# Four modulation halves summed on VectorE: from column-by-column accumulation to dot products along the partition

## The chip, the cores and the metric

The kernel runs on one core of a Trainium2 chip. The metric is device time in microseconds (us) of one execution. TensorE (PE in the rows, PEld for its weight loads), VectorE (DVE), ScalarE (ACT), GpSimd (POOL) and SyncE (SP, which here issues most of the DMAs) run side by side and wait for each other through semaphores.

## The reference, cut to what matters

A two-layer model on 256 tokens of width 1024. Each layer's norms and residuals are scaled by six vectors of length 1024 that come from one condition vector `c` through a 1024 x 6144 matrix:

```python
c_act = jax.nn.silu(c)
for l in range(DEPTH):
    mod = c_act @ mod_w[l] + mod_b[l]
    sh1, sc1, g1, sh2, sc2, g2 = jnp.split(mod[:, None, :], 6, axis=-1)
    hm = rmsnorm(x, norm_mix_g[l]) * (1.0 + sc1) + sh1
    y = mixer_hgrn2_shortconv(hm, ...) if l % 2 == 0 else mixer_nsa(hm, ...)
    x = x + g1 * y
    hf = rmsnorm(x, norm_ffn_g[l]) * (1.0 + sc2) + sh2
    x = x + g2 * conv_ffn(hf, ...)
return rmsnorm(x, final_norm_g)
```

Everything is float32. Each of the six vectors is 1024 dot products of length 1024, from 4 MB of weights. The program makes one vector at a time, by a function called `mod_half`, so a half here means one such vector. The change concerns four of the twelve: layer 0's `g2`, layer 1's `sc1` and `g1`, and layer 1's `sh2`.

## The kernel before

Activations lie transposed, 8 tiles of 128 features by 256 tokens. All large weights stream through one ring of six 1 MB buffers (`raw_w`, `raw_m`), loaded by SP in the order in which the program uses them; a load is issued when a buffer comes free. A weight matrix product is done in three passes: ScalarE rounds the weights to a high part (`whi`, L156), VectorE subtracts to get the low part (`wlo`, L165), and TensorE multiplies high by high, high by low and low by high (L417, tile `pg`). The splits run up to three sub-tiles ahead of the matmuls. The feed-forward of layer 0 (`ffn`, about 170 to 361 us) is 22 such "up" groups and four "down" groups; the attention of layer 1 (about 365 to 506 us) has its own sequence.

Work that is not part of these products stands in a list, `side`, of small functions. At every sub-tile `slot()` adds a credit (0.6 in the up groups, 1.2 in the down groups) and runs one function for each whole credit. The order of all engines follows from the order in which the program calls things.

A modulation half is made by `mod_half` in one of two ways. With `on_pe=True`, TensorE multiplies the activated condition with the weights (L289, tile `pm`), ScalarE copies the row of sums (L316), four transposes turn it into columns (L321) and VectorE adds the bias (L325, L327). With `on_pe=False`, eight VectorE instructions accumulate weight rows times the condition into `macc`, 128 partitions x 1024 columns (L299 for the first, L301 for the seven others). Then two matmuls with a column of ones add the 128 partitions up (`sums`, L309), and the same row copy (here 64 partitions), four transposes and bias add follow. In `side` that is 8 + 2 empty + `sums`, `rows`, empty, `turn`, `add`: 15 entries. Three halves of this kind stand in the feed-forward of layer 0 (L944), the fourth in the attention (L1288), where the eight steps are called at the iterations 15 to 19 of its loop (1, 1, 2, 2, 2) and the rest between the last output groups (L1330).

At the program's start TensorE runs five warm-up matmuls (`warm`, L627, each two records in the profile), then the first modulation column (L342), then the sums of squares (L484) of the input `xT` that arrives by DMA. `ident`, the identity for transposes, is a part of `kf`, loaded by the first DMA on ScalarE's queue (L240).

Of the kernel before, what the change touches and what calls it, by code (L numbers as in the profile page):

```python
# [38 lines left out]
WARM = (5, 1, 3)  # L39
# [160 lines left out]
def model(ctx, tc, xt, pack, wts, rel_bias, k_f, k_mask, k_hot, out, plan, got):  # L200
# [60 lines left out]
    ccol = one.tile([P, KD], F32, name="ccol")  # L261
    table(AF.Silu)
# [7 lines left out]
    def mod_half(l, qa, qb, on_pe=True, sums_in=None, tag="m"):  # L270
# [22 lines left out]
        def dve_step(j, e):  # L293
            if e == 0:
                s_["r"] = load(j)
            raw = s_["r"]
            if j + e == 0:
                s_["a"] = sums_in()
                dve.tensor_scalar(s_["a"], raw[:, 0, :], ccol[:, 0:1], None, op0=OP.mult)  # L299
            else:  # L300
                dve.scalar_tensor_tensor(s_["a"], raw[:, e, :], ccol[:, 2 * j + e:2 * j + e + 1], s_["a"], op0=OP.mult,  # L301
                                         op1=OP.add)
            if e == 1:
                st.done(s_["i"])

        def sums():
            s_["p"] = ps.tile([P, 512], "pm", "m")
            for q in range(2):
                pe.matmul(s_["p"][32 * q:32 * q + 32, :], one32, s_["a"][:, q * 512:(q + 1) * 512],  # L309
                          start=True, stop=True, skip_group_check=True, tile_position=(0, 32 * q))  # L310

        n = P if on_pe else 64

        def rows():
            s_["w"] = tmp.tile([P, 512], F32, name="mrow", bufs=1)
            act.activation(s_["w"][:n], s_["p"][:n], AF.Copy)  # L316

        def turn():
            s_["t"] = ps.tile([P, 4, P], "pm2", "m")
            for i in range(4):  # L320
                pe.transpose(s_["t"][:, i, :n], s_["w"][:n, i * P:(i + 1) * P], ident[:n, :n])  # L321

        def add():
            pv = s_["t"].rearrange("p j (e q r) -> p e q j r", q=2, r=32)
            dve.tensor_tensor(dst, pv[:, 0, :, :, 0], bias, op=OP.add)  # L325
            if on_pe:
                dve.tensor_tensor(dst, pv[:, 1, :, :, 0], dst, op=OP.add)  # L327
        if on_pe:
            return [lambda j=j: pe_step(j) for j in range(4)] + [rows, nop, turn, add]
        return [lambda j=j, e=e: dve_step(j, e) for j in range(4) for e in range(2)] + [nop] * 2 + [sums, rows, nop, turn, add]  # L330
# [476 lines left out]
    for b in (4, 6, 8):  # L807
        side.extend(mod_half(0, b, b + 1))
# [75 lines left out]
    ffp = [None]  # L884

    def ffn(l, H, rest, extra=None):
        with tc.tile_pool(name=f"ff{l}", bufs=1) as ff:
            ffp[0] = ff
# [54 lines left out]
    for l, b in ((0, 5), (1, 1), (1, 2)):  # L943
        side.extend(mod_half(l, 2 * b, 2 * b + 1, False, lambda: ffp[0].tile([P, 1024], F32, name="macc", bufs=1)))  # L944
# [242 lines left out]
    gT = tmp.tile([48, S], F32, name="gT", tag="m1k", bufs=1)  # L1187
# [9 lines left out]
    hid = tmp.tile([P, 256], F32, name="hid", tag="m1k", bufs=1)  # L1197
# [17 lines left out]
    hT = tmp.tile([P, 2, P], F32, name="hT", bufs=1)  # L1215
    dve.tensor_copy(hT, pt[:, :256].rearrange("p (j n) -> p j n", j=2))
    hv = tmp.tile([P, 2, 4, 4, 16], F32, name="hv", bufs=1)
# [20 lines left out]
    v4 = tmp.tile([64, 4, 64], F32, name="v4", tag="m1k", bufs=1)  # L1238
# [20 lines left out]

    def late_sums():  # L1260
        return ns.tile([P, 4, 400], F32, name="macc", tag="FDM", bufs=2).rearrange("p a n -> p (a n)")[:, :D]
# [3 lines left out]
    for n in range(NH + 6):  # L1265
# [21 lines left out]
        if n == M_AT:  # L1287
            mods = [f for f in mod_half(1, 6, 7, False, late_sums) if f is not nop]  # L1288
# [43 lines left out]
    gap.extend(mod_half(1, 10, 11, True))  # L1332
# [42 lines left out]
def lay_out(inp, plan):  # L1375
# [18 lines left out]
    for kind, off, n, what in plan[0]:  # L1394
        dst = wts[off:off + P * n]
        if what[0] == "mod":
# [42 lines left out]
```

## Time and profile before

| | us |
|---|---|
| median of 3 runs | 704.21 (703.83 to 705.22) |
| the profiled execution | 708.95 |
| its span, to which the rows' times refer | 707.1 |

| engine | busy share of the span |
|---|---|
| TensorE, matmuls | 98% |
| TensorE, weight loads | 90% |
| VectorE | 69% |
| ScalarE | 53% |
| GpSimd | 7% |

The page gives busy time by engine, the chain of work that ended last, groups of instructions by line, and DMA issues; the trace is read further by stretches of time, by instruction and by waits. An instruction's duration includes its tail, in which the next one may already run, so the distance between two starts is shorter than the duration. Times in rows count from the start of the span.

### The profile page before, as it was taken

The numbers are of one execution on the slowest core, as the hardware profiler recorded it, in microseconds if no ns is written. First come the engines' busy times: TensorE is split into PE (matmuls) and PEld (weight loads), VectorE is DVE, ScalarE is ACT, GpSimd is POOL, SyncE is SP. The second block draws the span as 40 slices with busy tenths as digits, with TensorE's granted clock in tenths as the row PEclk, the third lists the DMA queues.
The fourth block names the chain that finished last, engine by engine and source line by source line (L and its number), as shares of the span: only waits on it lengthen the run. The fifth ranks groups of instructions, "written<-read, shape, count | busy, mean of one in ns | idle before, by whom it ended". The sixth has DMA issues, their size and how long they took to land.

```text
span 707.1 us, 14267 instructions
## 1 busy us (share of the span) xinstructions
PE 692.3 (98%) x5866; PEld 637.1 (90%) x5866; DVE 487.1 (69%) x887; ACT 377.1 (53%) x646; POOL 48.1 (7%) x80
## 2 busy tenths in 40 slices
PE   7999999999999999999999999999999999999996
PEld 4889897887999999999989799878789999999996
DVE  2667675548689868969568767788686776775552
ACT  5446235535655555444346668784466555564452
POOL 0000000000000000000010015665000000000000
PEclk8999999999999999999999999999999999999999
DMA  8995657887658856769768482516677555455301
GB/s 332 416 420 211 259 187 251 321 317 285 230 185 296 309 181 246 283 233 337 284 239 319 191 341 81 205 49 224 243 280 266 190 208 199 164 173 193 127 1 60
DMA packets 27794, 165.12 MB, mean 233 GB/s; under 512 B 3258, under 2 KB 3770, under 8 KB 10320
## 3 DMA queue, kind: packets, MB, share of 16 engines
q1 hardware_dynamic: 26352, 159.94, 61.0%
q0 software_dynamic: 944, 3.60, 1.5%
q8 instruction: 46, 0.75, 0.4%
q10 hardware_dynamic: 432, 0.66, 0.2%
q14 instruction: 20, 0.16, 0.1%
HBM read 163.10 MB, written 1.08 MB: 232 GB/s over the span
## 4 chain that ended last, share of the span: by engine, by line
PE 89%; DVE 3%; ACT 3%; DMA 2%; issue 1%; POOL 0%; SPq 0%; ACTq 0%
PE pg L417 74%; PE pm L289 3%; PE pl L726 2%; DMA raw_w<-in_wts_dram 1%; PE pn L484 1%; PE p L1036 1%; DVE wlo L165 1%; PE po L1066 1%; PE pc L1174 1%; PE pm L342 1%; DMA xT<-in_xt_dram 1%; PE sc L988 1%; ACT whi L156 1%; ACT E L1020 1%; PE pm L309 1%
## 5 line engine op out<-in xcount | busy, mean ns | idle before, releaser
L165 DVE TENSOR_TENSOR wlo<-raw_w,whi 128x1024 fp32r<-128x1024 f32 (+1 forms) x194 | 226.3, 1173 | 136.2 <-ACT whi L156 127.4
L417 PE MATMUL pg<-hhi,whi 128*128 128x256 f32 x1096 | 295.8, 284 | 0.1
L417 PE MATMUL pg<-hlo,whi 128*128 128x256 f32 x1096 | 289.1, 278 | 0.0
L417 PE MATMUL pg<-hhi,wlo 128*128 128x256 f32 x1096 | 286.1, 278 | 0.0
L156 ACT ACTIVATE whi<-raw_w 128x1024 fp32r<-128x1024 f32 (+1 forms) x194 | 196.1, 1018 | 146.3 <-PE pg L417 116.9
L417 PEld LDWEIGHTS pg<-hhi,whi 128*128 128x128 f32 x1096 | 200.3, 189 | 19.2 <-issue 12.5
L417 PEld LDWEIGHTS pg<-hlo,whi 128*128 128x128 f32 x1096 | 199.5, 188 | 0.0
L417 PEld LDWEIGHTS pg<-hhi,wlo 128*128 128x128 f32 x1096 | 198.6, 189 | 0.0
L417 PE MATMUL pg<-Ah,whi 128*128 128x256 f32 x352 | 97.9, 278 | 0.0
L417 PE MATMUL pg<-Ah,wlo 128*128 128x256 f32 x352 | 97.2, 276 | 0.0
L417 PE MATMUL pg<-Al,whi 128*128 128x256 f32 x352 | 97.2, 276 | 0.0
L417 PEld LDWEIGHTS pg<-Ah,whi 128*128 128x128 f32 x352 | 66.1, 188 | 1.8 <-ACT whi L156 1.7
L417 PEld LDWEIGHTS pg<-Al,whi 128*128 128x128 f32 x352 | 66.1, 188 | 0.0
L417 PEld LDWEIGHTS pg<-Ah,wlo 128*128 128x128 f32 x352 | 66.1, 188 | 0.0
L1027 POOL TENSOR_SCALAR E<-E,rr,gr 128x128 f32<-128x128 f32 (+1 forms) x64 | 41.1, 657 | 31.0 <-DVE rr L1025 22.7
L902 DVE SCALAR_TENSOR_TENSOR tt<-pg,pk,tt 128x255 f32<-128x255 f32 (+1 forms) x88 | 36.2, 473 | 2.9 <-ACT tt L898 2.9
L912 ACT ACTIVATE Ah<-tt 128x512 fp32r<-128x512 f32 x22 | 13.9, 633 | 44.5 <-DVE tt L911 44.5
L301 DVE SCALAR_TENSOR_TENSOR macc<-raw_m,ccol,macc 128x1024 f32<-128x1024 f32 x28 | 35.9, 1283 | 0.1
L529 ACT ACTIVATE hhi<-xn,modc 128x256 fp32r<-128x256 f32 x31 | 15.1, 507 | 25.0 <-DVE xn L528 25.0
L1020 ACT ACTIVATE E<-E,mx 128x128 f32<-128x128 f32 (+1 forms) x64 | 28.2, 445 | 0.0
L289 PE MATMUL pm<-raw_m,cst 128*32 128x512 f32 x192 | 27.1, 642 | 0.0
L557 DVE SCALAR_TENSOR_TENSOR xT<-pg,modc,xT 128x256 f32<-128x256 f32 x32 | 14.1, 476 | 9.6 <-PE pg L417 9.5
(233 smaller groups left out, 787.3 us busy)
## 6 DMA issues: line engine op xcount, KB each, us to landing
raw_w<-in_wts_dram SPq DMA_DIRECT2D x84, 1024.0 KB, 4.9
raw_m<-in_wts_dram SPq DMA_DIRECT2D x52, 1024.0 KB, 6.6
raw_e<-in_wts_dram SPq DMA_DIRECT2D x24, 256.0 KB, 8.6
raw_w<-in_wts_dram SPq DMA_DIRECT2D x8, 768.0 KB, 4.9
FDM<-ub POOLq DMA_DIRECT2D x4, 800.0 KB, 7.9
raw_w<-in_wts_dram SPq DMA_DIRECT2D x5, 512.0 KB, 5.3
xT<-in_xt_dram SPq DMA_DIRECT2D x3, 256.0 KB, 6.4
out_dram<-yo ACTq DMA_DIRECT2D x2, 256.0 KB, 2.8
```

The lines of the kernel that those rows point to most:

```text
L156: self.nc.scalar.activation(hi, raw, AF.Copy)
L165: self.nc.vector.tensor_tensor(lo, raw, hi, op=OP.subtract)
L289: pe.matmul(s_["p"][o:o + 32, :], cst[:, 2 * j + e, :], raw[:, e, q * 512:(q + 1) * 512], start=(j == 0), stop=(j == 3), skip_group_check= ...
L301: dve.scalar_tensor_tensor(s_["a"], raw[:, e, :], ccol[:, 2 * j + e:2 * j + e + 1], s_["a"], op0=OP.mult, op1=OP.add)
L417: pe.matmul(o, a, b, start=self.first[i], stop=False, skip_group_check=True)
L529: act.activation(hi[:, k, :], xs[k], AF.Identity, bias=B[:, k:k + 1])
L557: dve.scalar_tensor_tensor(xT[:, k, :], src, g[:, k:k + 1], xT[:, k, :], op0=OP.mult, op1=OP.add)
L726: pe.matmul(pp[:, hd, :], lhs[:, hd, ls * P:(ls + 1) * P], rhs[:, hd, rs * P:(rs + 1) * P], start=True, stop=True)
L902: dve.scalar_tensor_tensor(tt[:, m, d:], acc[:, m, :S - d], w_fc[l][:, c:c + 1], tt[:, m, d:], op0=OP.mult, op1=OP.add)
L912: act.activation(Ah[:, sl, :], tt, AF.Copy)
L1020: act.activation(o, o, AF.Exp, bias=E["mx"][:, t, br:br + 1], scale=-1.0, accum_out=E["den"][:, t, br:br + 1])
L1027: pool.tensor_scalar(o, o, rr[:, t, br:br + 1], gr4[:, t, 1 + br, n:n + 1], op0=OP.mult, op1=OP.mult)
```

## The change

The four halves with `on_pe=False` are replaced by `mod_dots`. The weights of these halves are laid out transposed on the host: a partition holds whole columns of the matrix, 1024 elements each, so that one VectorE instruction, `tensor_tensor_reduce`, multiplies such a column with the condition vector, adds the products up along the partition, starts from the bias and writes one column of `modc`. Eight instructions make a half. Each is two instructions for the engine: the product and sum, and a read of the accumulator. The `sums`, `rows`, `turn` and `add` of these halves are gone, and so are `macc` and the empty entries: 8 entries in `side` instead of 15.

For this the condition must lie on every partition as a row of 1024 (`cb`). Eight transposes of a broadcast column, at the very start, and two ScalarE copies make it. The first group of warm-up matmuls goes from five to three. Five small tiles of the attention that shared one buffer (`m1k`) or had their own in `tmp` move to the four buffers of tag `T`.

```diff
-WARM = (5, 1, 3)
+WARM = (3, 1, 3)
...
+    cb = one.tile([P, D], F32, name="cb")
...
-        return [lambda j=j, e=e: dve_step(j, e) for j in range(4) for e in range(2)] + [nop] * 2 + [sums, rows, nop, turn, add]
+    def mod_dots(l, q):
+
+        s_ = {}
+
+        def dot(j, e):
+            if e == 0:
+                s_["i"] = st.load("m", 2048, "dots", l, 512 * q + 256 * j)
+            raw = st.raw(s_["i"])[:, e * D:(e + 1) * D]
+            n = 4 * q + 2 * j + e
+            dve.tensor_tensor_reduce(raw, raw, cb, scale=1.0, scalar=modb[l][:, n:n + 1], op0=OP.mult, op1=OP.add,
+                                     accum_out=modc[l][:, n:n + 1])
+            if e == 1:
+                st.done(s_["i"])
+        return [lambda j=j, e=e: dot(j, e) for j in range(4) for e in range(2)]
...
+    pcb = [ps.tile([P, 4, P], "pcb", "g") for _ in range(2)]
+    for k in range(KD):
+        pe.transpose(pcb[k // 4][:, k % 4, :], ccol[:, k:k + 1].to_broadcast([P, P]), ident)
+    for h in range(2):
+        act.activation(cb[:, h * 512:(h + 1) * 512], pcb[h].rearrange("p k n -> p (k n)"), AF.Copy)
     warm(WARM[0])
...
-    for l, b in ((0, 5), (1, 1), (1, 2)):
-        side.extend(mod_half(l, 2 * b, 2 * b + 1, False, lambda: ffp[0].tile([P, 1024], F32, name="macc", bufs=1)))
+    for l, q in ((0, 10), (1, 2), (1, 4)):
+        side.extend(mod_dots(l, q))
...
-    gT = tmp.tile([48, S], F32, name="gT", tag="m1k", bufs=1)
+    gT = ns.tile([48, S], F32, name="gT", tag="T", bufs=4)
...
-            mods = [f for f in mod_half(1, 6, 7, False, late_sums) if f is not nop]
+            mods = mod_dots(1, 6)
...
+        if what[0] == "dots":
+            _, l, c0 = what
+            dst.reshape(P, 2, D)[...] = f["mod_w"][l][:, c0:c0 + 2 * P].T.reshape(2, P, D).transpose(1, 0, 2)
```

On TensorE, in the feed-forward of layer 0, this is the place between two up groups where the first half's sums stood (`pg` is a group's accumulator, `hhi` and `hlo` the activations; the numbers are the buffers'). Before:

```order
L417 MATMUL pg_2797<-hlo_1937,whi_2729 128x256
L417 MATMUL pg_2797<-hhi_1936,wlo_2730 128x256
L309 MATMUL pm_2873<-macc_2369,one32_131 32x512 x2
L417 MATMUL pg_2798<-hhi_1936,whi_2768 128x256
L417 MATMUL pg_2798<-hlo_1937,whi_2768 128x256
```

and after:

```order
L409 MATMUL pg_2807<-hlo_1948,whi_2739 128x256
L409 MATMUL pg_2807<-hhi_1947,wlo_2740 128x256
L409 MATMUL pg_2808<-hhi_1947,whi_2778 128x256
L409 MATMUL pg_2808<-hlo_1948,whi_2778 128x256
L409 MATMUL pg_2808<-hhi_1947,wlo_2779 128x256
```

The next group now follows directly; nothing else is in a different order on TensorE there. The four transposes of L321 go in the same way at each half's later place.

On VectorE, at the first two steps of the same half (`tt` and `Al` belong to the feed-forward's own gating), before:

```order
L165 TENSOR_TENSOR wlo<-raw_w,whi 128x1024
L299 TENSOR_SCALAR macc<-raw_m,ccol 128x1024
L165 TENSOR_TENSOR wlo<-raw_w,whi 128x1024
L911 TENSOR_TENSOR tt<-pg,tt 128x512
L301 SCALAR_TENSOR_TENSOR macc<-raw_m,ccol,macc 128x1024
L165 TENSOR_TENSOR wlo<-raw_w,whi 128x1024
```

and after:

```order
L165 TENSOR_TENSOR wlo<-raw_w,whi 128x1024
L318 ISA raw_m,modc_81<-raw_m,cb,pk 128x1024
L318 ISA modc_81 128x1
L165 TENSOR_TENSOR wlo<-raw_w,whi 128x1024
L905 TENSOR_TENSOR tt<-pg,tt 128x512
L318 ISA raw_m,modc_81<-raw_m,cb,pk 128x1024
L318 ISA modc_81 128x1
L165 TENSOR_TENSOR wlo<-raw_w,whi 128x1024
```

Each step became a pair in the same place (L318 is `tensor_tensor_reduce`, with the accumulator read behind it). The steps of the second and third half move up, since the seven other entries between the halves are gone: all 24 now stand inside the up groups.

On ScalarE at the start, before:

```order
L264 ACTIVATE ccol<-pk 128x8
L245 ACT_TABLE_LOAD
L245 ACTIVATE scr<-epsc 128x1
L634 ACTIVATE qf<-xT 128x512 x2
L634 ACTIVATE tq<-xT 128x512
```

and after:

```order
L265 ACTIVATE ccol<-pk 128x8
L245 ACT_TABLE_LOAD
L245 ACTIVATE scr<-epsc 128x1
L625 ACTIVATE cb<-pcb 128x512 x2
L632 ACTIVATE qf<-xT 128x512 x2
```

The two copies of the condition stand ahead of the squares of the input.

## Rows read from the trace of the kernel before

**Rows 1.** The page: engines' busy time; shares of the chain that ended last.

```profile
PE 692.3 (98%) x5866; PEld 637.1 (90%) x5866; DVE 487.1 (69%) x887; ACT 377.1 (53%) x646; POOL 48.1 (7%) x80
...
PE 89%; DVE 3%; ACT 3%; DMA 2%; issue 1%; POOL 0%; SPq 0%; ACTq 0%
```

**Rows 2.** Chain that ended last, in order of time (start us, us, what): L309.

```profile
246.13 0.98 PE pm L309 x4
...
502.18 0.98 PE pm L309 x4
```

**Rows 3.** The same chain, asked narrowly around two halves: the transposes.

```profile
255.79 0.39 PE pm L321 x4
...
504.74 0.39 PE pm L321 x4
```

**Rows 4.** Stretches: us, PE, PEld, DVE, ACT, POOL busy (count), PEclk, DMA share, GB/s.

```profile
206.10:240.60 34.50, 34.50 (x295) 34.50 (x295) 30.34 (x38) 18.59 (x25) 0.00 (x0) 1.00 0.76 278
...
314.00:332.00 18.00, 18.00 (x161) 18.00 (x160) 17.21 (x18) 7.86 (x9) 0.00 (x0) 1.00 0.84 313
...
475.90:496.80 20.90, 20.75 (x189) 18.18 (x188) 18.15 (x31) 9.02 (x22) 11.11 (x12) 1.00 0.58 207
```

**Rows 5.** VectorE groups by line and shape: busy us, mean ns | idle before.

```profile
L165 DVE TENSOR_TENSOR wlo<-raw_w,whi 128x1024 fp32r<-128x1024 f32 x176 | 214.1, 1223 | 130.6 <-ACT whi L156 122.0 <-PE pm L321 3.6 <-PE pm L289 3.1
L301 DVE SCALAR_TENSOR_TENSOR macc<-raw_m,ccol,macc 128x1024 f32<-128x1024 f32 x28 | 35.9, 1283 | 0.1
...
L299 DVE TENSOR_SCALAR macc<-raw_m,ccol 128x1024 f32<-128x1024 f32 x4 | 3.0, 740 | 0.0
```

**Rows 6.** VectorE in order of time (start us, us): `tensor_tensor_reduce` in attention.

```profile
472.16 0.29 DVE L1008 CUSTOM_DVE_ANT_0 E<-sc,FDM 128x128 f32<-128x128 f32 x1
...
472.37 0.42 DVE L1008 CUSTOM_DVE_ANT_0 E<-sc,FDM 128x256 f32<-128x256 f32 x1
472.71 0.08 DVE L1008 DVE_READ_ACCUMULATOR2_ANT mx<- 128x1 f32 x1
472.71 0.42 DVE L1008 CUSTOM_DVE_ANT_0 E<-sc,FDM 128x256 f32<-128x256 f32 x1
```

**Rows 7.** VectorE in order of time: the attention's half, first and last steps.

```profile
475.93 0.72 DVE L299 TENSOR_SCALAR macc<-raw_m,ccol 128x1024 f32<-128x1024 f32 x1
477.29 1.22 DVE L165 TENSOR_TENSOR wlo<-raw_w,whi 128x1024 fp32r<-128x1024 f32 x1 [0.64 <-ACT whi L156]
...
492.62 2.60 DVE L301 SCALAR_TENSOR_TENSOR macc<-raw_m,ccol,macc 128x1024 f32<-128x1024 f32 x2
495.13 1.28 DVE L165 TENSOR_TENSOR wlo<-raw_w,whi 128x512 fp32r<-128x512 f32 x2
496.34 0.41 DVE L1053 COPY Tc<-p 64x256 f32<-64x256 f32 x1
```

**Rows 8.** TensorE in order of time, behind those steps.

```profile
496.80 1.08 PE L1091 MATMUL po<-Tc,vc 64*64 64x256 f32 x8 [0.15 <-DVE Tc L1053]
```

**Rows 9.** The chain's first piece.

```profile
2.59 6.63 DMA xT<-in_xt_dram
```

**Rows 10.** TensorE in order of time, at the start.

```profile
3.12 4.05 PE L627 MATMUL pw<-kk,cst 128*32 128x256 f32 x9 [3.12 <-ACT cst L263]
...
10.20 0.44 PE L353 MATMUL pm<-kf,mrow 128*128 128x128 f32 x2 [0.54 <-ACT mrow L348]
```

**Rows 11.** ScalarE in order of time, at the start.

```profile
7.93 1.28 ACT L634 ACTIVATE qf<-xT 128x512 f32<-128x512 f32 x2 [3.26 <-DMA xT<-in_xt_dram]
```

**Rows 12.** The row copies' line: ns min/median/max, first and last start, shapes.

```profile
L316 ACT ACTIVATE mrow<-pm x10: 574/581/600, 99.6 to 532.9; 128x512 f32<-128x512 f32 x6, 64x512 f32<-64x512 f32 x4
```

**Rows 13.** DMA issues: count, KB each, us to landing.

```profile
kf<-in_k_f_dram ACTq DMA_DIRECT2D x1, 130.5 KB, 2.3
```

**Rows 14.** Stretches at the start, columns as in rows 4.

```profile
11.00:12.00 1.00, 1.00 (x7) 0.92 (x6) 0.55 (x5) 0.00 (x0) 0.00 (x0) 0.51 1.10 449
...
17.50:18.00 0.50, 0.50 (x4) 0.50 (x5) 0.50 (x2) 0.00 (x0) 0.00 (x0) 0.66 0.91 377
```

More of the change, by code (lines that the diff above doesn't have):

```diff
@@ L268, in nop, with mod_half @@
         pass
-    def mod_half(l, qa, qb, on_pe=True, sums_in=None, tag="m"):
+    def mod_half(l, qa, qb, tag="m"):
         def cols(t):
@@ L291, in pe_step @@
             st.done(s_["i"])
[L293 to L312, printed above, removed]
         def rows():
             s_["w"] = tmp.tile([P, 512], F32, name="mrow", bufs=1)
-            act.activation(s_["w"][:n], s_["p"][:n], AF.Copy)
+            act.activation(s_["w"], s_["p"], AF.Copy)
         def turn():
@@ L320, in turn @@
             for i in range(4):
-                pe.transpose(s_["t"][:, i, :n], s_["w"][:n, i * P:(i + 1) * P], ident[:n, :n])
+                pe.transpose(s_["t"][:, i, :], s_["w"][:, i * P:(i + 1) * P], ident)
         def add():
@@ L325, in add @@
             dve.tensor_tensor(dst, pv[:, 0, :, :, 0], bias, op=OP.add)
[L326 to L329, printed above, removed]
-        return [lambda j=j, e=e: dve_step(j, e) for j in range(4) for e in range(2)] + [nop] * 2 + [sums, rows, nop, turn, add]
+            dve.tensor_tensor(dst, pv[:, 1, :, :, 0], dst, op=OP.add)
+        return [lambda j=j: pe_step(j) for j in range(4)] + [rows, nop, turn, add]
+    def mod_dots(l, q):
[10 more added lines that the diff above has]
+        return [lambda j=j, e=e: dot(j, e) for j in range(4) for e in range(2)]
     def first_scales(c, A, gb):
@@ L806, in model @@
     after = [None]
-    for b in (4, 6, 8):
-        side.extend(mod_half(0, b, b + 1))
+    side.extend(mod_half(0, 4, 5) + mod_half(0, 6, 7) + mod_half(0, 8, 9))
     side[:0] = [nop] * 3
@@ L1196, in model @@
         pe.transpose(pt3[:, t * 64:t * 64 + 48], gT[:, (1 - t) * P:(2 - t) * P], ident[:48, :48])
-    hid = tmp.tile([P, 256], F32, name="hid", tag="m1k", bufs=1)
+    hid = ns.tile([P, 256], F32, name="hid", tag="T", bufs=4)
     act.activation(hid, pc[:, :256], AF.Silu)
@@ L1331, in model @@
             mods.pop(0)()
-    gap.extend(mod_half(1, 10, 11, True))
+    gap.extend(mod_half(1, 10, 11))
     out_tail(G[3], [G[3].sub(6, 2, HELD_NSA[3])], g1)
@@ L1395, in lay_out @@
         dst = wts[off:off + P * n]
-        if what[0] == "mod":
+        if what[0] == "dots":
+            _, l, c0 = what
+            dst.reshape(P, 2, D)[...] = f["mod_w"][l][:, c0:c0 + 2 * P].T.reshape(2, P, D).transpose(1, 0, 2)
+        elif what[0] == "mod":
             _, l, k, nk, starts, w = what
```

10 lines of the change are left out of this document (3 added, 7 removed).

## Prediction

> **What bounds the kernel now.** I read the page first: TensorE is busy 98% of the span and carries 89% of the chain of work that ended last [rows 1]. So an instruction on TensorE is worth its own time wherever TensorE has no gap, and one on VectorE (69%) or ScalarE (53%) is worth nothing until somebody waits for it. Then the chain in order of time, for the pieces that the change removes: each of the four halves is in it twice, with its two matmuls of sums for 0.98 us and with its four transposes for 0.39 us, of which the first and the last stand here [rows 2, 3]. Last, the stretches in which the eight VectorE steps of a half run. In 206.1 to 240.6 TensorE is busy 34.50 of 34.50 us although VectorE is busy 30.34; in 314 to 332 it is still 18.00 of 18.00 with VectorE at 17.21 of 18 [rows 4]. In the attention, 475.9 to 496.8, TensorE loses 0.15 us, and that one gap ends with VectorE [rows 4, 8].
>
> **What is removed from TensorE.** Four times 0.98 + 0.39 = 5.48 us. These pieces lie between dense matmuls: in the feed-forward no gap stands on either side, so the next group's matmuls start earlier by the whole amount if its weights are split by then. The splits run up to three sub-tiles ahead and TensorE doesn't wait for them in these stretches, so I count all of it: **-5.48 us**. The four row copies (0.58 us each, [rows 12]) and four small adds vanish from ScalarE and VectorE; nobody on the chain waits for them, so they count nothing.
>
> **What VectorE does instead.** The old steps are one L299 and seven L301, 0.72 us and, start to start, 1.26 us (492.62 to 495.13 is two of them) [rows 5, 7]; with the add, about 9.6 us a half. The new instruction of this size is not in the trace. The nearest row is the same instruction in the attention, with a different pair of operations and one source in PSUM: 0.21 us from start to start at 128 columns, 0.34 at 256, and the accumulator read starts together with the next product, so it adds nothing [rows 6]. That is about 1.05 ns a column: 0.34 + 768 x 0.00105 = 1.15 us at 1024 columns, 9.2 us a half. The other end is L301's pace plus a whole accumulator read, 1.26 + 0.08 = 1.34 us, 10.7 us a half. I take 1.15, since it comes from the same instruction.
>
> In the feed-forward this changes a half by -0.4 to +1.1 us in a stretch with 4.2 us of VectorE idle [rows 4], and TensorE runs up to three sub-tiles behind the splits: **0 us**. What is new there is that the three halves follow each other without a pause, 24 steps in a row. Since one half at this density cost no TensorE time, and 314 to 332, in which VectorE was 96% busy, cost none either, I expect no debt to pile up. If the cover went, the price would be the overrun of VectorE. The loads come denser too, with the same bytes: the dense stretch moves 278 GB/s and the one at 314 to 332 313 GB/s, both without a gap on TensorE [rows 4]. A load of weights that is queued on SP behind a load of the modulation would be what is late; no row shows it late at these rates.
>
> In the attention the steps stay at their places. The first grows from 0.72 to 1.15 or 1.34 us, and the split behind it waited 0.64 us for ScalarE anyway [rows 7]. The last four stand right before the splits and the copy `Tc` that TensorE waited for at 496.80. At 1.15 they end earlier and win back at most that 0.15 us; at 1.34 the four add 0.3 us on TensorE's path. I take **0**, with -0.15 to +0.3 as bounds.
>
> **The start.** Two warm-up matmuls less are four records; nine took 4.05 us, tail included, so about 0.43 each and 1.7 us less [rows 10]. Eight transposes are added: at the price of the four in the feed-forward (0.39 us for 64 rows, [rows 3]) 0.8 us, at that of L353 (two in 0.44 us with the tail, [rows 10]) 1.8 us. So TensorE's block at the start moves by -0.9 to +0.1 us. It is under cover in any case: the chain there is the DMA of `xT`, which lands at 9.22 [rows 9], and TensorE has 0.54 us of idle before 10.20 [rows 10]. The two copies into `cb` cost ScalarE two times 0.58 us ([rows 12], the same shape) and stand ahead of the squares, but ScalarE idles 3.26 us there before the input lands [rows 11]. The transposes wait for `kf`: it takes 2.3 us to land [rows 13] as the first transfer on its queue, about when the old warm-up began (3.12, [rows 10]). If it landed late, the copies would first use up ScalarE's 2.1 us of spare idle, and only then push the squares. **0 us**, with bounds of -0.5 and +1.
>
> The renaming of five small tiles in the attention only changes buffers; `hid` no longer waits for the reads of `gT`. TensorE is the chain there and nothing waits for `hid` at once: 0.
>
> **The sum.** -5.48 + 0 + 0 + 0 = -5.5 us on a span of 707.1. The profiled execution took 708.95 us, its span and 1.85 us around it, and the median of the runs is 704.21, 4.7 us below; I carry that distance over unchanged: 704.21 - 5.5 = **698.7 us**.
>
> **Rivals.**
>
> *The new instruction runs at half pace.* Both its sources lie in SBUF as float32, and it sums while it multiplies; the instruction of [rows 6] has one source in PSUM, so the trace doesn't show this combination. For it speaks that L301, with two float32 sources in SBUF, is slower than the subtraction L165 (1283 against 1223 ns, [rows 5]); against it, that this is 5%, not double. Half pace is another 1024 x 1.05 ns: 2.23 us a step, 0.97 more than L301. In the dense stretch eight steps add 7.8 us where 4.2 are idle, an overrun of 3.6 us a half and 10.8 us for three, of which the lead of three sub-tiles (about 8 us) can hide a part once: 2.5 to 10.8 us. In the attention 8 x 0.97 + 0.5 = 8.2 us meet 2.75 us of idle [rows 4]: 5.5 us. Sum: -5.5 + 5.5 + (2.5 to 10.8), **about 710 us, slower**. It decides from roughly 1.8 us a step (1.26 + 4.2/8), and the sum is positive from about 2.1.
>
> [...]
>
> *The gain comes back as a wait in the feed-forward.* The denser steps or loads make one split late per group, TensorE waits instead of multiplying the sums, and only the attention's half or less is won: **about 703.5 us**. For it: VectorE at 88% and DMA at 0.76 over 103 us instead of 35. Against it: the gapless 314 to 332 [rows 4].
>
> [...]
>
> **Chances.** Forecast 0.76 at 698.7 (its own terms span 697.5 to 700.1); clock for the worse 0.07, for the better 0.04; gain comes back 0.06; half pace 0.07. Range: 696.9 to 702.0, which takes in the forecast with its bounds and both clock cases and leaves out 0.13 and the edges. About 0.2%, 1.4 us, is what a measurement of this kernel can tell from no change. Faster by more than that (below 702.8): 0.76 + 0.07 + 0.04 = 0.87 and a little of the gain that comes back, 0.88; same 0.05; slower 0.07.
>
> **What would show it.** No `pm` matmuls from ones and no 64-row transposes in the chain, and TensorE still gapless in the feed-forward. VectorE's new instruction at 1.15 to 1.34 us from start to start; above 1.8 the forecast falls. In the attention, no wait above 0.5 us on VectorE at the copy `Tc`. At the start the squares still begin when `xT` lands, and the first `pg` matmul stands near 17.2 us. A first `pg` matmul later than 18.5, or gaps on TensorE ended by `wlo` or `raw_w` in the feed-forward, would make the prediction wrong.

## The result and the profile after

| | before | after |
|---|---|---|
| median, first comparison | 704.02 us (702.63 to 705.22) | 695.02 us (693.98 to 697.17) |
| the profiled execution | 708.95 us | 697.17 us |
| its span | 707.1 us | 695.4 us |

The ratio is 0.986, 95% interval 0.9826 to 0.9895: faster by 9.0 us by the medians, where the prediction had 5.5, and 1.9 us below the low end of its range. The changed kernel was measured unchanged in two later batches, on two chips: 697.4 (ratio 0.9901, 0.9881 to 0.9920) and 699.2 (0.9921, 0.9895 to 0.9947). Over all 22 runs of the three its median is 697.4, and single runs lie between 694.0 and 702.6; over all 132 runs of before that stood beside the experiments the median is 704.5. So the change is worth about 7 us, and the first four runs lay on the favourable side of its spread, by luck. Medians and ranges here leave out five runs over 1.5% above the fastest of their kernel, one of them of 1144.8 us at a granted clock of 0.56.

Of the changed kernel, the page's lines that answer to [rows 1]:

```profile
PE 680.7 (98%) x5838; PEld 631.4 (91%) x5838; DVE 489.2 (70%) x915; ACT 375.4 (54%) x644; POOL 48.4 (7%) x80
...
PE 90%; DVE 4%; ACT 3%; DMA 1%; issue 0%; POOL 0%; SPq 0%; ACTq 0%
```

TensorE is still the bound. The chain that ended last, in the feed-forward of layer 0 (start us, us, what; the dense matmuls are L409 now, L417 before):

```profile
168.60 13.94 PE pg L409 x120
...
183.53 8.38 PE pg L409 x72
...
192.35 157.78 PE pg L409 x1392
```

Where the pieces of [rows 2, 3] stood, 1392 matmuls follow each other without a gap, 157.78 / 1392 = 113.3 ns from start to start. TensorE waits for none of the 24 dot products. The same chain in the attention, where the last two dots and a split stand ahead of the copy `Tc`, the place of [rows 7, 8]:

```profile
482.29 0.96 DVE raw_m L318
...
483.49 1.20 DVE raw_m L318
...
484.70 1.20 DVE wlo L165 x2
485.90 0.34 DVE Tc L1047
...
486.29 1.08 PE po L1085 x8
487.37 8.36 PE pg L409 x72
495.73 1.00 PE pm L290 x8
```

TensorE takes up `Tc` at 486.29 without a wait that the profile lists; before it waited 0.15 us there [rows 8].

The dot products by their line (ns min/median/max, first and last start, shapes):

```profile
L318 DVE CUSTOM_DVE_ANT_0 raw_m<-raw_m,cb,pk x32: 1251/1278/1317, 203.4 to 483.4; 128x1024 f32<-128x1024 f32 x32
L318 DVE DVE_READ_ACCUMULATOR2_ANT modc<- x32: 75/82/89, 204.7 to 484.6; 128x1 f32 x32
```

A dot takes 1.20 us from start to start (483.49 to 484.70 in the chain), and the accumulator read starts with the next instruction and adds nothing. The start, TensorE in order of time, answers to [rows 10]:

```profile
3.29 1.97 PE L623 MATMUL pcb<-kf,ccol 128*128 128x128 f32 x8 [3.29 <-ACT ccol L265]
...
16.99 1.22 PE L409 MATMUL pg<-hhi,whi 128*128 128x256 f32 x4
```

and ScalarE there, to [rows 11]:

```profile
4.65 1.23 ACT L625 ACTIVATE cb<-pcb 128x512 f32<-128x512 f32 x2
7.91 1.28 ACT L632 ACTIVATE qf<-xT 128x512 f32<-128x512 f32 x2 [2.02 <-DMA xT<-in_xt_dram]
```

The squares start at 7.91 (7.93 before), when the input lands; the first dense matmul stands at 16.99 (17.22 before). In these two executions the start is unchanged, with a granted clock of 0.50 from 12 to 17 us in both.

### Where the profiled execution's 11.7 us went

Pieces of the chain of before that stood between those of [rows 2, 3] (start us, us, what):

```profile
170.24 14.90 PE pg L417 x120
...
186.13 8.68 PE pg L417 x72
...
195.24 50.88 PE pg L417 x432
...
247.11 8.69 PE pg L417 x72
...
303.62 5.66 PE pg L417 x48
...
309.67 24.69 PE pg L417 x216
...
497.88 4.30 PE pg L417 x36
...
503.17 1.58 PE pg L417 x12
...
505.13 2.93 PE pg L417 x24
508.06 0.99 PE pm L289 x8
```

*A switch to each removed piece and back.* 48 matmuls at 113.3 ns are 5.44 us, the piece at 303.62 takes 5.66; 216 are 24.47, the piece at 309.67 takes 24.69. A dense piece between two others is 0.22 us longer than its matmuls. TensorE in order of time around the sums at 246 shows where:

```profile
245.84 0.28 PE L417 MATMUL pg<-hhi,wlo 128*128 128x256 f32 x1
246.06 1.05 PE L309 MATMUL pm<-macc,one 128*32 128x512 f32 x4
247.04 0.39 PE L417 MATMUL pg<-hhi,whi 128*128 128x256 f32 x1
247.26 0.29 PE L417 MATMUL pg<-hlo,whi 128*128 128x256 f32 x1
```

From the last dense matmul to the sums, and again from the first dense one behind them to the second, it is 0.22 us instead of 0.12: about 0.1 us for the switch and as much for the way back. Around the transposes at 255.72 it is the same. Each half has two such interruptions: 0.98 + 0.39 + 2 x 0.22 = 1.81 us, not 1.37. The attention agrees: from 497.88 to the end of the last row it is 11.17 us, in the changed kernel 9.36 from 487.37 to the end of its `pm` row, 1.81 apart.

*Another pace.* 432 matmuls in 50.88 us are 117.8 ns each, 4.5 ns more than in those 1392 of the changed kernel. The four slower pieces (14.90, 8.68, 50.88, 8.69) are 0.96, 0.30, 1.91 and 0.31 us longer than the changed kernel's at 113.3 ns: 3.5 us. In `b_again`, before once more, the first of them takes 14.45 at the same pace, with a granted clock of 1.00 from 167 to 173 us, where before's is 0.89 in 171 to 173; so 0.45 of this is put down to the clock and 3.0 to the pace.

*The norm ahead of it.* The first `pg` matmul of the feed-forward stands at 168.60 instead of 170.24: 1.6 us. Before had a granted clock of 0.50 in 169 to 171 us of this execution, the changed kernel 1.00 (below): with the 0.45 of the first dense matmuls, 2.1 us.

4 x 1.81 + 3.0 + 2.1 = 12.3 us; small differences of either sign take back 0.6. Only the first of these is work that the change removes. The experiments tell the three apart.

### The profile page after: what moved, and what is told of

Same layout as the page of the kernel before. It is cut to its first block, busy times and chain, and to the rows that moved or that the text cites. A ratio compares the mean times of both kernels' runs of the same rounds, so it can differ in the third digit from the quotient of the medians.

```text
span 695.4 us, 14229 instructions
## 1 busy us (share of the span) xinstructions
PE 680.7 (98%) x5838; PEld 631.4 (91%) x5838; DVE 489.2 (70%) x915; ACT 375.4 (54%) x644; POOL 48.4 (7%) x80
## 4 chain that ended last, share of the span: by engine, by line
PE 90%; DVE 4%; ACT 3%; DMA 1%; issue 0%; POOL 0%; SPq 0%; ACTq 0%
PE pg L409 75%; PE pm L290 3%; PE pl L724 2%; PE pn L476 1%; PE p L1030 1%; DVE wlo L165 1%; PE po L1060 1%; PE pc L1168 1%; PE pm L334 1%; DMA xT<-in_xt_dram 1%; PE sc L982 1%; ACT whi L156 1%; ACT E L1014 1%; PE pw L619 1%; DVE Q L968 0%
## 5 line engine op out<-in xcount | busy, mean ns | idle before, releaser
L409 PE MATMUL pg<-hhi,whi 128*128 128x256 f32 x1096 | 293.7, 282 | 0.7 <-ACT whi L156 0.5
L409 PE MATMUL pg<-hlo,whi 128*128 128x256 f32 x1096 | 287.9, 277 | 0.0
L409 PE MATMUL pg<-hhi,wlo 128*128 128x256 f32 x1096 | 285.0, 277 | 0.0
L409 PEld LDWEIGHTS pg<-hhi,whi 128*128 128x128 f32 x1096 | 199.4, 188 | 16.9 <-issue 10.9
L409 PEld LDWEIGHTS pg<-hlo,whi 128*128 128x128 f32 x1096 | 199.0, 188 | 0.0
L409 PEld LDWEIGHTS pg<-hhi,wlo 128*128 128x128 f32 x1096 | 198.0, 188 | 0.0
L409 PE MATMUL pg<-Ah,whi 128*128 128x256 f32 x352 | 97.4, 277 | 0.0
L409 PE MATMUL pg<-Ah,wlo 128*128 128x256 f32 x352 | 97.2, 276 | 0.0
L409 PE MATMUL pg<-Al,whi 128*128 128x256 f32 x352 | 97.2, 276 | 0.0
L409 PEld LDWEIGHTS pg<-Ah,whi 128*128 128x128 f32 x352 | 66.1, 188 | 0.0
L409 PEld LDWEIGHTS pg<-Al,whi 128*128 128x128 f32 x352 | 66.1, 188 | 0.0
L409 PEld LDWEIGHTS pg<-Ah,wlo 128*128 128x128 f32 x352 | 66.1, 188 | 0.0
L318 DVE CUSTOM_DVE_ANT_0 raw_m<-raw_m,cb,pk 128x1024 f32<-128x1024 f32 x32 | 40.6, 1278 | 0.0
L898 ACT ACTIVATE tt<-tt 128x512 f32<-128x512 f32 x22 | 14.0, 635 | 19.9 <-DVE tt L896 18.8
```

The source lines that it names most:

```text
L318: dve.tensor_tensor_reduce(raw, raw, cb, scale=1.0, scalar=modb[l][:, n:n + 1], op0=OP.mult, op1=OP.add, accum_out=modc[l][:, n:n + 1])
L409: pe.matmul(o, a, b, start=self.first[i], stop=False, skip_group_check=True)
L898: defer(taps, lambda: act.activation(tt, tt, AF.Silu))
```

## The experiments

### What the removed work is worth, and the dots

Before, unchanged, for the spread:

> The kernel before, once more, for its spans and a second trace. Theory 'pace': in the first trace the dense matmuls of the feed-forward of layer 0 ran at 117.8 ns each from 172 to 256 us and at 113.3 ns after that, in the changed kernel at 113.3 ns all through; if that slow pace belongs to the kernel, it is there again and the time stays near 704. Theory 'chance': the slow pace followed a load that landed late at 158 us and a fall of the granted clock at 168 us, and is gone in this trace, with a time near 700 to 701.

Measured: 704.7 us (702.6 to 708.4), ratio 1.0002 (0.9977 to 1.0028).

Before without the sums, rows, transposes and add of the four halves (their result is left out, only the bias is written); the eight old steps stay:

```diff
-        return [...] + [nop] * 2 + [sums, rows, nop, turn, add]
+        return [...] + [nop] * 5 + [nop, bias_only]
```

> The kernel before without sums, row copy, transposes and bias add of the four VectorE halves (their columns get the bias alone, so those four vectors of the output are left out); the VectorE steps, the loads and the empty entries stay. Theory 'removal': all of the gain is TensorE work that is gone, so this gains as much as the changed kernel, -8 to -9 us (5.5 us of rows, the rest pace and switching). Theory 'dots': a part of the gain comes from the new VectorE form and its place, and this gains only 5.5 to 6.5 us.

Measured: 698.8 us (696.4 to 704.1), ratio 0.9926 (0.9895 to 0.9957). Taking TensorE's work away, with the old steps on VectorE, gives the change's gain as far as these intervals can tell.

The changed kernel with seven empty entries behind each half's dots in the list, so that these start at the old distance:

```diff
-        side.extend(mod_dots(l, q))
+        side.extend(mod_dots(l, q) + [nop] * 2 + [idle, idle, nop, idle, idle])
```

> The changed kernel with as many entries in the list as before (seven that do nothing behind each of the three halves of the feed-forward), so that the steps and loads of the second and third half stand as late as before. Theory 'removal': no change against the changed kernel, 695 us within 1. Theory 'place': the gain beyond 5.5 us came from the steps that moved up, so this loses 2 to 3.5 us of it, 697 to 698.5.

Measured: 699.7 us, single runs from 694.7 to 705.0, ratio 0.9935 (0.9898 to 0.9972). This can't tell the two theories apart. The spread is the point; it is taken up below.

The changed kernel with the removed work of TensorE put back at its old places and its result thrown away: `spare` holds two matmuls of 64 rows, the row copy, four 64-row transposes and a copy.

```diff
-        side.extend(mod_dots(l, q))
+        side.extend(mod_dots(l, q) + spare())
...
-            mods = mod_dots(1, 6)
+            mods = mod_dots(1, 6) + [f for f in spare() if f is not nop]
```

> The changed kernel with the removed TensorE work put back at its old places for all four halves: two matmuls with ones (of the condition row, thrown away), the row copy of 64 partitions, four transposes, one small VectorE copy. Theory 'removal': everything is lost again, 704 us. Theory 'rows': it costs the 5.5 us that the rows show, 700.5 us, and the other 3.5 us came from elsewhere (start, dots, their place).

Measured: 711.2 us, ratio 1.0096 (1.0064 to 1.0128): slower than before, which none of the theories had. A second batch:

> The changed kernel with the removed work of TensorE put back at its old places (results thrown away), once more for a second profile: it took 711.2 us where before takes 704.6 with the same number of matmuls. 'Chance': a load of 10 us and an unlucky run of paces stood in the first profile; a second batch gives 702 to 707. 'Dots': the dot products delay something that only shows beside the interruptions (a split late behind a dot at an interruption): again 708 to 715, and the profile shows waits on VectorE or on raw_w in layer 0's feed-forward that before doesn't have. 'Pace': again 708 or more, without waits, with the slower pace in most pieces between interruptions.

Measured: 710.8 us (709.6 to 711.6), ratio 1.0089 (1.0066 to 1.0112). Chance was out; both profiles are alike, with no wait in the feed-forward. All dense matmuls that read `Ah`, `Al`, `ohi` or `olo` ran at 118.3 ns, from the first one on and without an interruption ahead of it (the 216 that take 24.69 us in before take 25.75 in the chain of `a_back`). What differs there from the kernels above is an address: the 32 bytes of the small thrown-away tile had moved `Ah` from byte 145408 of the partition to 145440, and the other three with it, as all tiles allocated behind it. `hhi` and `hlo` stand ahead of it and did not move.

### A tile's address

The tile of `a_back` made 64 bytes wide:

```diff
-            o = tmp.tile([P, 2, 4], F32, name="spr", bufs=1)
+            o = tmp.tile([P, 2, 8], F32, name="spr", bufs=1)[:, :, :4]
```

> The kernel a_back once more, with one thing changed: its small thrown-away tile is 64 bytes wide on each partition instead of 32. The 32 bytes had moved every tile allocated behind it, Ah and Al of both feed-forwards and ohi and olo of the first mixer among them, to addresses that are 32 above a multiple of 64, and the dense matmuls that read these four run at 118.3 instead of 113.3 ns in both profiles of a_back. 'Address': 1056 matmuls with Ah or Al and 192 with ohi or olo, 5.0 ns each, are 6.2 us that go: 711 becomes 704 to 706, the time of before (704.6), and the four tiles' matmuls run at 113.3. 'Dots beside interruptions' (the dot products cost what a_back shows): again 710 to 711.

Measured: 713.7 us, ratio 1.0109 (1.0068 to 1.0150): not what 'address' said. `Ah` now stands at 145472, and its matmuls take 120.0 ns. A multiple of 64 is not enough here; which addresses are good isn't settled, only that at 145408 the matmuls took 113.3 ns.

The changed kernel with nothing but a tile of 32 bytes:

```diff
+    skew = tmp.tile([P, 8], F32, name="skew", bufs=1)
...
+        dve.memset(skew, 0.0)
```

> The changed kernel with one unused tile of 32 bytes a partition, cleared once, and nothing else: Ah, Al, ohi and olo move by 32 bytes. 'Address': their 1248 matmuls take 118.3 instead of 113.3 ns, +6.2 us on the changed kernel's 697.4: 703.6, with the down groups of both feed-forwards at 118.3 and the up groups at 113.3. 'No address': 697.4 +- 1.

Measured: 704.4 us (703.2 to 708.4), ratio 0.9981 (0.9954 to 1.0009): 7.0 us above the changed kernel's 697.4, where 703.6 was expected. The whole gain of the change is gone through 32 bytes.

The work put back once more, its small tile laid into `mrow`, so that no other tile moves:

```diff
-            o = tmp.tile([P, 2, 4], F32, name="spr", bufs=1)
+            o = s_["w"][:, :8].rearrange("p (q j) -> p q j", q=2)
```

> The kernel a_back with its small thrown-away tile laid into a buffer that is there already, so that no other tile moves: Ah, Al, ohi and olo stand where they stand in the kernel before. (In a_back they stand 32 bytes higher and their matmuls run at 118.3 ns, in a_back3 64 bytes higher and at 120.0, in the changed kernel at 113.3.) 'Address': the 1248 matmuls are back at 113.3 and the time is that of before, 704.4 +- 1.5; its distance to the changed kernel is then the price of the removed work, 7.2 us by 1.80 us a half, 5.5 by the prediction's 1.37. 'Dots beside interruptions': 711 or more in spite of the addresses.

Measured: 704.3 us (703.7 to 705.8), ratio 0.9999 (0.9985 to 1.0013). With the work back the changed kernel takes before's time to 0.15%. So the form of the halves on VectorE, their place, the copies at the start and the renamed tiles are together worth nothing that can be measured, and the removed work is worth the whole change. One reservation: in the only profile of `a_back4` the up groups ran at 113.3 ns, in both of before the first 696 matmuls ran at 117.8, and what the other runs had isn't recorded. The next reading does not depend on that.

Its size can be read from the down groups of layer 0's feed-forward, which ran at one pace in all of these: TensorE's matmuls with `Ah` there (xcount: ns min/median/max, first and last start), of the changed kernel,

```profile
L409 PE MATMUL pg<-Ah,whi x176: 276/276/276, 290.1 to 349.6; 128*128 128x256 f32 x176
```

of before,

```profile
L417 PE MATMUL pg<-Ah,whi x176: 276/276/385, 297.0 to 360.1; 128*128 128x256 f32 x176
```

of `a_back4`,

```profile
L434 PE MATMUL pg<-Ah,whi x176: 276/276/385, 292.3 to 355.4; 128*128 128x256 f32 x176
```

of `a_back`,

```profile
L434 PE MATMUL pg<-Ah,whi x176: 277/281/388, 293.5 to 359.1; 128*128 128x256 f32 x176
```

of `a_back3`,

```profile
L434 PE MATMUL pg<-Ah,whi x176: 278/283/386, 297.4 to 363.8; 128*128 128x256 f32 x176
```

and of `a_skew`.

```profile
L409 PE MATMUL pg<-Ah,whi x176: 277/280/285, 292.9 to 355.1; 128*128 128x256 f32 x176
```

First to last start is 59.5 us in the changed kernel and 63.1 in before and in `a_back4`: 3.6 us for the two halves whose sums and transposes lie there, 1.80 each. The 385 ns are the first matmuls behind an interruption, which the changed kernel doesn't have. The last three rows show the address: 65.6, 66.4 and, without the removed work, 62.2 us, with medians of 280 to 283 ns instead of 276.

### The pace

> The changed kernel once more, unchanged, for two theories of the 3.5 us that it won beyond the 5.5 of the sum. 'Draw': the dense matmuls of layer 0's feed-forward run at 113.3 or at 117.8 ns from start to start, the pace is taken at an interruption and kept until the next, and the changed kernel has no interruption there for 1392 matmuls, so one draw decides over 1392 x 4.5 ns = 6.3 us: its runs lie in two heaps, about 694 to 697 and 699 to 704, the median anywhere between (697 to 700), and the profile's first pg of layer 0's feed-forward to its first matmul of the down groups takes 121.5 or 126.2 us. 'Kernel': the four runs at 694.0 to 697.2 are what the kernel takes; median 695 +- 1, ratio 0.987, and no run above 699.

Measured: 697.4 us (696.8 to 698.4), ratio 0.9901 (0.9881 to 0.9920): neither two heaps nor 695. A third measurement had single runs from 694.3 to 702.6 and a median of 699.2 (ratio 0.9921, 0.9895 to 0.9947, which holds 0.990 and not 0.986):

> The changed kernel a third time, so that the kernel a_g2 has it beside it on the same chip, and for its distance to before. By the price of the removed work, 1.80 us a half by the down groups, 7.2 us in all: 697.2, ratio 0.990. By the first comparison (695.0 against 704.0): 0.986.

The three profiles of the changed kernel all show 157.78 us for the 1392 matmuls. `a_nops`, which has the same order on TensorE there, has this row in its chain:

```profile
193.05 163.95 PE pg L412 x1392
```

163.95 / 1392 = 117.8 ns, 6.2 us more, and `b_nosum`'s profile shows 163.95 too; its ten runs lie in two heaps, six at 696.4 to 699.0 and four at 703.1 to 704.1, the profiled one among the four. A stretch of `a_nops` (columns as in [rows 4])

```profile
200.00:240.00 40.00, 40.00 (x342) 40.00 (x341) 36.40 (x54) 21.53 (x29) 0.00 (x0) 1.00 0.74 264
```

beside the same of the changed kernel

```profile
200.00:240.00 40.00, 40.00 (x355) 40.00 (x354) 37.29 (x55) 21.06 (x28) 0.00 (x0) 1.00 0.78 278
```

shows what the pace is not: the granted clock is 1.00 and TensorE is busy throughout in both. Only the count differs, 342 and 355. What chooses the pace was tried with four 64-row transposes, thrown away, as interruptions at three places of the changed kernel:

```diff
+    for i in (8, 4, 0):
+        side.insert(len(side) - 24 + i, stir)
```

> The changed kernel with four transposes of 64 rows (thrown away) at three places early in layer 0's feed-forward: ahead of the first, fifth and ninth dot. Their own price by the chain of before is 3 x 0.39 = 1.2 us, by the distance from the last pg before to the second pg after them 3 x 0.59 = 1.8 us. 'Draw': each interruption draws the pace anew, so the 1392 matmuls are cut in four with the last the longest; the two heaps move closer or blur, and the median is that of the changed kernel of this batch +1.2 to +1.8, with single profiles that change between 113.3 and 117.8 ns at one of the three places and nowhere else. 'Kernel' (the slower pace comes from what VectorE or the loads do, not from the interruption): pace as in the changed kernel, time +1.2, no change of pace at the three places.

Measured: 698.0 us (696.7 to 699.3), ratio 0.9909 (0.9889 to 0.9928), 0.6 above the changed kernel beside it. Its chain (start us, us, what; L312 are the added transposes):

```profile
191.60 16.96 PE pg L414 x144
208.56 0.39 PE pm L312 x4
208.95 19.25 PE pg L414 x168
228.20 0.39 PE pm L312 x4
228.59 16.53 PE pg L414 x144
```

144 matmuls take 16.96 us ahead of the first interruption (117.8 ns) and 16.53 behind the second (113.3 ns and the 0.22 us of the switches): the pace changed at the first. That looked like a way to reset it, and before got the same at two places early in its first half:

```diff
+    for i in (6, 3):
+        side.insert(base + i, stir)
```

> The kernel before with four 64-row transposes (thrown away) at two places early in layer 0's feed-forward, behind the third and the fifth step of its first half, and nothing else. 'Pace': both profiles of before run the up groups at 117.8 ns until the first half's own 64-row transposes, some 690 matmuls, and at 113.3 behind them; the new ones bring that forward by about 400 to 450 matmuls, -1.9 us, for a price of 2 x 0.6 to 0.8: -0.3 to -0.7 us, and the first of them is where the pace changes in the profile. 'Place' (the pace changes at the half's end for another reason): +1.2 to +1.6 us and the change of pace where it was.

Measured: 706.1 us (704.6 to 707.8), ratio 1.0020 (1.0006 to 1.0034): 1.6 slower, where two interruptions cost 2 x (0.39 + 0.22) = 1.2 us by the rows: no gain from the pace. Its chain (L273 are the added ones):

```profile
192.99 21.78 PE pg L422 x192
214.76 0.39 PE pm L273 x4
215.16 17.16 PE pg L422 x144
232.32 0.39 PE pm L273 x4
232.71 19.25 PE pg L422 x168
```

21.78 / 192 is 113.4 ns, then 117.8, then 113.3: the first interruption began the slow pace and the second ended it. So in these profiles the pace changed either way where other matmuls stand between the dense ones, and it held in every piece from one such place to the next, 1392 matmuls long in the changed kernel; what decides it stayed open. The old halves interrupt this feed-forward six times, so before can change its pace six times more; the changed kernel keeps one for 158 us. None of its own profiles caught the slow one; that some of its slower runs are of that kind is inferred from `a_nops` and `b_nosum`, not shown.

The granted clock is a second source of spread. In the norm ahead of the feed-forward, two stretches of the third measurement's profile (columns as above),

```profile
165.00:167.00 2.00, 2.00 (x14) 1.85 (x17) 0.07 (x1) 0.74 (x4) 0.00 (x0) 0.55 0.83 336
167.00:169.00 2.00, 2.00 (x10) 0.29 (x2) 0.17 (x1) 0.98 (x2) 0.00 (x0) 0.50 0.92 373
```

and of the first,

```profile
165.00:167.00 2.00, 2.00 (x19) 1.20 (x18) 0.28 (x3) 1.40 (x4) 0.00 (x0) 1.00 0.97 340
167.00:169.00 2.00, 1.88 (x17) 0.75 (x14) 1.29 (x4) 1.29 (x3) 0.00 (x0) 1.00 1.01 406
```

show a granted clock of 0.55 and 0.50 in one execution and of 1.00 in the other, with the same small matmuls of the norm ahead. The first dense matmul stands at 171.09 instead of 168.60. Before had 0.76, then 0.50 in 167 to 171 in its profiled execution, and 1.00 in `b_again`.

The granted clock is low at two other places too. At the start it is 0.50 from 12 to 17 us in both profiles of the first comparison, and in 17 to 18 us 0.50 in the changed kernel and 0.58 in before, with the first `pg` matmul at 16.99 and 17.22. In the norm ahead of layer 1's feed-forward it is 0.58 in 499 to 502 us of the changed kernel's first profile, and in before 0.80 in 511 to 514 and 0.64 in 514 to 517. Why the clock falls in one execution and not in the other was not tried. That the time up to the feed-forward differs as well, `a_turn` shows: its program is the changed kernel's up to the first added transposes, and its second dense piece there stands at 182.48 instead of 183.53.

### More halves in the same way

If a half is worth 1.8 us, further halves, those that TensorE multiplies in eight fp32 matmul steps, might be worth more. In all of these, twelve thrown-away matmuls (`fillers`) stay in the norm's gap. Three more, two of them in layer 0's feed-forward:

```diff
-    gaps = [mod_half(1, 8, 9), []]
-    for l, q in ((0, 10), (1, 2), (1, 4)):
+    gaps = [fillers(), []]
+    for l, q in ((0, 10), (1, 2), (1, 4), (1, 0), (1, 8)):
...
-    gap.extend(mod_half(1, 10, 11))
+    gap.extend(fillers())
+    side.extend(mod_dots(1, 10))
```

> The changed kernel with three more halves made by dot products, those of layer 1 that TensorE multiplies in the gaps of its norms; their matmuls, copies, transposes and adds are gone, and 12 matmuls (thrown away) stay in each of the gaps to keep TensorE at work there. 24 more dots on VectorE, 16 of them in layer 0's feed-forward, where 24 stand now, and 8 ahead of layer 1's feed-forward. If VectorE stays cover (1.20 us a dot; 40 dots x 1.20 = 48 us in a stretch of 170 us): each half takes about 20 matmuls less from TensorE's gaps, -1 to -2 us each, -3 to -6 in sum, 690 to 693 where the changed kernel takes 695. If the gaps are as long without this work (they end with the norm, not with TensorE): 0, within 1 us of the changed kernel. If VectorE or the loads become the bound: slower, with waits on wlo or raw_w in the feed-forward.

Measured: 701.2 us, ratio 0.9952 (0.9928 to 0.9976), slower than the changed kernel beside it (697.4). Its dots at the end of the attention stand on the chain, ahead of the last residual, and its up groups ran at 117.8 ns. With those dots moved into layer 1's feed-forward:

```diff
-    side.extend(mod_dots(1, 10))
...
+    side.extend(mod_dots(1, 10))
     ffn(1, nh, rest, (gains, turns))
```

> The kernel a_more with the dots of the last half (layer 1's g2) moved from the end of the attention into layer 1's feed-forward, where VectorE has no dots and g2 is needed only in the down groups. a_more took 701.2, and by its profile it loses 2 to 3 us at the end of the attention against the changed kernel, where two dots stand ahead of the last residual, and 5.9 us because its up groups of layer 0's feed-forward run 1321 matmuls at 117.8 ns. Expected: 698 to 699 if the slower pace comes again, 693 to 694 if not.

Measured: 699.8 us (697.3 to 705.1), ratio 0.9936 (0.9901 to 0.9971), its profile at 117.8 ns again. And with two interruptions added (`side.insert(i, stir)` at 6 and 3):

> The kernel a_late with four 64-row transposes (thrown away) at two places early in layer 0's feed-forward, behind the third and the fifth dot. In the traces so far, dense matmuls at 117.8 ns went back to 113.3 behind each such group of 64-row transposes (three of three) and stayed there behind them (all others). 'Pace reset': at the latest behind the second group the up groups run at 113.3; the two groups cost 0.6 to 0.8 us each, and about 130 matmuls at most stay slow (0.6 us): 694 to 696, below a_late where that has the slower pace. 'No reset': as a_late plus 1.4.

Measured: 702.4 us (701.5 to 708.1), ratio 0.9964 (0.9931 to 0.9996). Here the up groups ran at 113.3 ns, and TensorE waited in the down groups (who waited for whom: us in total, times, longest):

```profile
PE pg L425 <- DVE wlo L165: 3.9, 6, 0.8
...
PE pg L425 <- ACT whi L156: 2.2, 2, 1.5
```

The stretch of these waits

```profile
295.00:345.00 50.00, 43.95 (x366) 42.23 (x365) 43.78 (x62) 18.59 (x21) 0.00 (x0) 1.00 0.88 335
```

and the same of the changed kernel:

```profile
295.00:345.00 50.00, 50.00 (x444) 50.00 (x443) 32.89 (x41) 22.71 (x25) 0.00 (x0) 1.00 0.72 266
```

Five halves' loads keep the DMA at 0.88, ScalarE waited 22.4 us for `raw_w` in 280 to 345, and TensorE is busy 43.95 of 50 us. At the slower pace, in `a_late`, the same loads came in time for TensorE, which waited for none there. Four halves there and one in layer 1's feed-forward, without and with an interruption behind the third dot of each:

```diff
-    for l, q in ((0, 10), (1, 2), (1, 4)):
+    for l, q in ((0, 10), (1, 2), (1, 4), (1, 0)):
...
+    side.extend(mod_dots(1, 10))
     ffn(1, nh, rest, (gains, turns))
```

> The changed kernel with two more halves as dots: layer 1's first (its shift) behind the three in layer 0's feed-forward, and layer 1's g2 in layer 1's own feed-forward, each for its eight fp32 matmul steps on TensorE; twelve thrown-away matmuls stay in each norm's gap. From the profiles: layer 1's up groups took 122.5 us in the changed kernel and 120.6 where g2 was dots (a_more, a_best), layer 0's 121.5 to 122.1 against 119.5 (a_best without its transposes): -4 us where the pace is 113.3 and loads keep up, 691 to 694. With five halves there (a_best) TensorE waited 6 us for late splits in 295 to 345, at 335 GB/s; with four the list ends some 20 us earlier: 0 to 3 us of that left. With the slower pace over the whole feed-forward: +6.

> The kernel a_five with four 64-row transposes (thrown away) behind the third dot of each feed-forward, as a reset of the pace. 'Pace reset': its runs lie in one heap at a_five's faster runs +1.2 to 1.6; 'no reset': a_five's median +1.2 to 1.6.

Measured: 699.6 us (694.0 to 702.0), ratio 0.9917 (0.9882 to 0.9952), and 697.8 (695.3 to 699.6), ratio 0.9901 (0.9876 to 0.9927). Neither reached 691 to 694. Last, only the one half in layer 1's feed-forward:

> The changed kernel with one more half as dots: layer 1's g2, in layer 1's own feed-forward, where VectorE has no dots and g2 is needed only in the down groups; twelve thrown-away matmuls stay in the norm's gap. Nothing changes in layer 0's feed-forward, so the loads that made a_best and a_five late there don't come denser. From profiles: first pg to first Ah of layer 1 is 122.5 us in the changed kernel and 120.5 where g2 was dots (a_more, a_best, a_five): -2 us against a_third, 695. If that gain is taken back by the norm before it (its gap ends with VectorE and ScalarE): 0.

Measured: 700.5 us (693.0 to 700.8), ratio 0.9915 (0.9885 to 0.9945), beside 0.9921 of the changed kernel on the same chip: no difference. No version beat the changed kernel.

## Why the prediction was wrong

*What bounds the kernel* held: TensorE is the bound before and after, and the kernel got faster because it does less.

*"What is removed from TensorE"* failed in its size. The step took the pieces' own lengths from the chain, 0.98 + 0.39, and let the next group start earlier "by the whole amount". The switch to each piece and back costs another 0.22 us, which the sum put at nothing, so a half is 1.81 us and the term 7.2, not 5.48. The rows for it were in the same chain: the lengths of the dense pieces by their counts, which the prediction never divided.

*The range.* With the term at its size the sum gives 704.2 - 7.2 = 697.0, just inside the range, and over all its runs the changed kernel takes 697.4. That the first four runs gave 695.0 is luck, and the range was too narrow for such luck: the two paces were in neither a term nor a rival, and the clock had no more than the 0.07 and 0.04 of its two cases. The paces stood in [rows 4]: 295 matmuls in 34.50 us and 161 in 18.00, about 117 and 112 ns at the same clock and without a gap. The prediction read the busy times and not the counts. One pace or the other over the 1392 matmuls is 6.2 us, more than the range was wide. The first comparison's profiled execution had the quick pace and no fall of the clock in the norm of layer 0's feed-forward; the two later ones had the quick pace and the fall, and took 1.3 and 2.9 us longer. What the runs without a profile had isn't known, so the 2.0 us between 695.0 and the sum's 697.0 are put down to these two causes by size, not by a record of each run. The bounds that the prediction gives for its own terms add up to 698.1 to 700.0, not to 697.5 to 700.1; neither reaches 695.0.

*What VectorE does instead* held: 1.20 us a dot between the bounds of 1.15 and 1.34, no wait of TensorE in the feed-forward, and none at `Tc` in the attention that the profile shows. `a_back4` shows the term at 0. Its cover is not large: with five halves loads and splits come late (6.1 us of waits of TensorE in `a_best`).

*The start* held for the profiled executions of the first comparison, 16.99 against 17.22; the time up to the feed-forward's second dense piece moves by more from one execution to the next (182.48 in `a_turn`, 183.53 in the changed kernel).

*The rivals.* Half pace is refuted by 1.20 us, with two float32 sources in SBUF and an accumulator. The gain that comes back as a wait did not happen with three halves; with five it did (`a_best`), through loads. The clock at the start did not decide: both profiled executions of the first comparison had it at 0.50 from 12 to 17 us. No run shows what the range's two clock cases are worth; in their place the runs showed a first `pg` matmul at 16.99 and 17.22 with that clock.

## What to carry to other kernels

Divide each dense piece of the chain by its count before pricing what stands between the pieces: the quotient shows the pace, and what a piece has above it is the price of the switches (0.22 us here), which a removed interruption gives back with its own time. When a kernel changes, compare the addresses of the operands of its main matmuls first; an experiment that adds a tile of 32 bytes can cost as much as what it measures (7.0 us in `a_skew`). And here 1392 equal matmuls in a row took one of two paces to the end, 6.2 us apart, and in the norm ahead of them the granted clock was 0.50 in some executions and 1.00 in others: measure such a kernel more than once before trusting a per cent.

## What the runs showed of the hardware

- Dense 128x256 matmuls run at 113.3 or at 117.8 ns from start to start, both at the granted clock of 1.00; the pace was seen to change, in either direction, only where other matmuls stood between.
- Switching from the dense matmuls to float32 matmuls or transposes and back costs 0.22 us beside their own time, half on each side; the first dense matmul behind them takes 385 instead of 276 ns.
- In the norm ahead of layer 0's feed-forward the granted clock was 0.50 from 167 to 171 us in two of three profiles of the same kernel and 1.00 in the third, with the same small matmuls ahead; the first dense matmul then stood 2.4 to 2.5 us later.
- Matmuls that read `Ah` take 113.3 ns where it stands at 145408 bytes of the partition (the changed kernel), 118.3 at 145440 (`a_back`) and 120.0 at 145472 (`a_back3`).
- `tensor_tensor_reduce` on VectorE takes 1.20 us for 1024 float32 columns, its accumulator read of 82 ns hidden behind the next start.
